# Ending a copy kernel on TensorE in place of SyncE

## The chip, the cores and the metric

The kernel runs on one core of one Trainium2 chip. The metric is the device time of one execution in microseconds (us). The core has five engines that run programs of their own and meet only at semaphores: PE (TensorE), DVE (VectorE), ACT (ScalarE), POOL (GpSimd) and SP (SyncE). Copies are issued by an engine and carried out by 16 DMA engines.

## What is computed

The reference keeps the tokens whose position lies under a capacity and sets the others to zero:

```python
batch, seq, hidden, capacity = 16, 1024, 512, 256
x = np.random.randn(batch, seq, hidden).astype(np.float32)
token_positions = np.random.randint(0, capacity, (batch, seq)).astype(np.int32)

mask = token_positions < capacity
out = (x * mask[..., np.newaxis]).astype(np.float32)
```

`x` and the output have 16 x 1024 x 512 float32 values, 33.55 MB each. The positions of these inputs are all under the capacity, so no token is dropped and the output equals `x`.

## The kernel before

The 16,384 rows of 512 values are spread over 128 partitions of 128 rows each. The kernel copies all of `x` to the output at once, within HBM, and looks meanwhile whether any token has to be dropped.

*The copies (lines 72 to 94).* Eight DMAs of 4 MB each go from `x` to the output, issued in turn by SP and ACT, four by each; ACT first issues the load of the positions into `tp`. All eight count on one semaphore, `s_copy`, by 16 each, so it stands at 128 when all have landed. These issues are moved by hand to the head of the program, ahead of the start-up barriers.

*The check (lines 97 to 127).* DVE computes `keep`, one number of 1 or 0 for each token, from the two 32-bit halves of each position (`ge`, `lt`, `low`, `keep`), and sums it to `kept`. PE adds the 128 partial sums by one matmul with `ones` into `total`, and DVE turns that into `drop_i`: 1 if any token is dropped. The matmul is the only thing that PE does.

*The branch (lines 130 to 161).* SP, ACT and DVE load `drop_i` into a register and branch. If a token is dropped, they load, multiply and store everything again. With these inputs the branch is not taken.

*The end (lines 165 to 175).* [...] ACT and DVE add 1 to `s_done`; SP waits for 2 and adds 1; POOL waits for 3 and clears all of the kernel's semaphores other than `s_copy`. SP at last waits until `s_copy` has 128 and subtracts 128, in one instruction, which the profile books on line 175. No engine but SP waits for the copies on the path that is taken here; the other engines have ended their programs by then. There is no scheduler: the order on each engine is the order in which the code is written.

Of the kernel before, what the change touches and what calls it, by code (L numbers as in the profile page):

```python
# [1 line left out]

# [4 lines left out]


@with_exitstack
def kernel(  # L10
    ctx: ExitStack,
    tc: tile.TileContext,
    x: bass.AP,
    token_positions: bass.AP,
    capacity: bass.AP,
    out: bass.AP,
):
    nc = tc.nc
    P = nc.NUM_PARTITIONS
    fp32 = mybir.dt.float32  # L20
    i32 = mybir.dt.int32
    Alu = mybir.AluOpType

    x_f = x.flatten_outer_dims()
    out_f = out.flatten_outer_dims()
    N, D = x_f.shape
    n_per_p = N // P
    cap = float(int(capacity))
    x_r = x_f.rearrange("(p n) d -> p n d", p=P)
    out_r = out_f.rearrange("(p n) d -> p n d", p=P)  # L30
    tp_i32 = token_positions.rearrange("b s -> (b s)").bitcast(i32)

    sp = nc.sync
    act = nc.scalar
    ve = nc.vector
    pe = nc.tensor
    gp = nc.gpsimd


    tc.close()  # L40
    tc.compile()  # L41

    def sbuf(name, shape, dtype):
        return ctx.enter_context(nc.sbuf_tensor(name, shape, dtype)).ap()

    tp = sbuf("tp", [P, 2 * n_per_p], i32)
    ge = sbuf("ge", [P, n_per_p], fp32)
    lt = sbuf("lt", [P, n_per_p], fp32)
    low = sbuf("low", [P, n_per_p], fp32)
    keep = sbuf("keep", [P, n_per_p], fp32)  # L50
    kept = sbuf("kept", [P, 1], fp32)
    ones = sbuf("ones", [P, 1], fp32)
    drop_i = sbuf("drop_i", [1, 1], i32)
    total = ctx.enter_context(nc.psum_tensor("total", [1, 1], fp32)).ap()
    F = 16
    NBUF = 2
    n_fix = n_per_p // F
    xts = [sbuf(f"xt{b}", [P, F, D], fp32) for b in range(NBUF)]

    s_copy = nc.alloc_semaphore("s_copy")  # L60
    s_tp = nc.alloc_semaphore("s_tp")
    s_ve = nc.alloc_semaphore("s_ve")
    s_pe = nc.alloc_semaphore("s_pe")
    s_ld = [nc.alloc_semaphore(f"s_ld{b}") for b in range(NBUF)]
    s_mul = nc.alloc_semaphore("s_mul")
    s_st = [nc.alloc_semaphore(f"s_st{b}") for b in range(NBUF)]
    s_done = nc.alloc_semaphore("s_done")

    n_copy = 0
    early = []  # L70

    load_tp = act.dma_start(out=tp, in_=tp_i32.rearrange("(p w) -> p w", p=P))
    early.append(load_tp.then_inc(s_tp, 16).ins)

    C = 16
    for k in range(n_per_p // C):
        ins = (sp, act)[k % 2].dma_start(
            out=out_r[:, k * C : (k + 1) * C, :], in_=x_r[:, k * C : (k + 1) * C, :]  # L80
        ).then_inc(s_copy, 16)
        early.append(ins.ins)
        n_copy += 1


    home = nc.cur_bb.bb
    first_bb = nc.cur_f.blocks[0]
    first_sp = next(
        k for k, i in enumerate(first_bb.instructions) if i.engine == mybir.EngineType.SP
    )  # L90
    names = [i.name for i in early]
    home.instructions = [i for i in home.instructions if i.name not in names]
    first_bb.instructions = (
        first_bb.instructions[:first_sp] + early + first_bb.instructions[first_sp:]
    )

    lo = tp[:, 0 : 2 * n_per_p : 2]
    hi = tp[:, 1 : 2 * n_per_p : 2]


    ve.memset(ones, 1.0).then_inc(s_ve, 1)  # L101
    ve.wait_ge(s_tp, 16)
    ve.tensor_scalar(  # L103
        out=ge, in0=lo, scalar1=0.0, scalar2=None, op0=Alu.is_ge
    ).then_inc(s_ve, 1)
    ve.wait_ge(s_ve, 2)
    ve.scalar_tensor_tensor(  # L107
        out=lt, in0=lo, scalar=cap, in1=ge, op0=Alu.is_lt, op1=Alu.mult
    ).then_inc(s_ve, 1)
    ve.wait_ge(s_ve, 3)  # L110
    ve.scalar_tensor_tensor(  # L111
        out=low, in0=hi, scalar=0.0, in1=lt, op0=Alu.is_equal, op1=Alu.mult
    ).then_inc(s_ve, 1)
    ve.wait_ge(s_ve, 4)
    ve.scalar_tensor_tensor(  # L115
        out=keep, in0=hi, scalar=0.0, in1=low, op0=Alu.is_lt, op1=Alu.add
    ).then_inc(s_ve, 1)
    ve.wait_ge(s_ve, 5)
    ve.tensor_reduce(  # L119
        out=kept, in_=keep, axis=mybir.AxisListType.X, op=Alu.add  # L120
    ).then_inc(s_ve, 1)
    pe.wait_ge(s_ve, 6)
    pe.matmul(out=total, lhsT=ones, rhs=kept, start=True, stop=True).then_inc(s_pe, 1)  # L123
    ve.wait_ge(s_pe, 1)
    ve.tensor_scalar(  # L125
        out=drop_i, in0=total, scalar1=float(N) - 0.5, scalar2=None, op0=Alu.is_lt
    ).then_inc(s_ve, 1)


    for e in (sp, act, ve):  # L130
        e.wait_ge(s_ve, 7)
    ET = mybir.EngineType
    drop = nc.values_load(
        drop_i[0:1, 0:1],
        engines=[ET.SP, ET.Activation, ET.DVE],
        min_val=0,
        max_val=1,
        skip_runtime_bounds_check_because="a comparison gives 0 or 1",
    )
    with nc.If(drop):  # L140
        for u in range(n_fix):
            b = u % NBUF
            if u >= NBUF:
                sp.wait_ge(s_st[b], 16 * (u // NBUF))
            sp.dma_start(out=xts[b], in_=x_r[:, u * F : (u + 1) * F, :]).then_inc(s_ld[b], 16)
            ve.wait_ge(s_ld[b], 16 * (u // NBUF + 1))
            for j in range(F):
                c = u * F + j
                ve.tensor_scalar(
                    out=xts[b][:, j, :],  # L150
                    in0=xts[b][:, j, :],
                    scalar1=keep[:, c : c + 1],
                    scalar2=None,
                    op0=Alu.mult,
                ).then_inc(s_mul, 1)
            if u == 0:
                act.wait_ge(s_copy, 16 * n_copy)
            act.wait_ge(s_mul, (u + 1) * F)
            act.dma_start(out=out_r[:, u * F : (u + 1) * F, :], in_=xts[b]).then_inc(s_st[b], 16)
        for b in range(NBUF):  # L160
            act.wait_ge(s_st[b], 16 * (n_fix // NBUF))

    for e in (act, ve):
        e.sem_inc(s_done, 1)
    sp.wait_ge(s_done, 2)
    sp.sem_inc(s_done, 1)
    own = [s_tp, s_ve, s_pe, *s_ld, s_mul, *s_st, s_done]
    ids = sorted(s.num for s in own)  # L170
    assert ids == list(range(ids[0], ids[-1] + 1))
    gp.wait_ge(s_done, 3)
    gp.sem_clear(range(ids[0], ids[-1] + 1))
    sp.wait_ge(s_copy, 16 * n_copy)
    sp.sem_inc(s_copy, -16 * n_copy)


# [1 line left out]
_INS = ['x', 'token_positions', 'capacity']  # L179
_OUTS = [((16, 1024, 512), 'float32')]  # L180

_NUMBERS = {'capacity': 256}


# [26 lines left out]
```

## Time and profile before

| what | value |
|---|---|
| median of 4 runs | 105.85 us (105.61 to 106.36) |
| profiled execution | 105.69 us |
| its span, first to last instruction of the program | 104.4 us |
| busy: PE, DVE, POOL | 0.2, 1.5 and 0.2 us |
| moved in HBM | 33.69 MB read, 33.55 MB written |
| mean granted TensorE clock | 1.000 |

The page counts only computing instructions as busy; issues of DMAs, branches and semaphore instructions are not in its table of groups, but stand in the views by line under names such as SPq or PEldq (the queue of an engine's sequencer; PEldq is PE's). Times inside the profile count from the first instruction of the program. What an engine does ahead of its program and behind it has no rows there; the trace keeps the updates of every semaphore, those too that fall outside the span.

### The profile page before, as it was taken

Reading aid. Unit: us, or ns where it says so; the run is one execution under the profiler, and the core shown is the slowest. Engines: PE = TensorE matmul, PEld = TensorE weight load, DVE = VectorE, ACT = ScalarE, POOL = GpSimd, SP = SyncE. Lnnn points to the kernel's source line nnn. Section 1 sums busy time; section 2 is a strip of 40 time slices with the busy share of each in tenths; the row PEclk is TensorE's granted clock in tenths of the full one; section 3 lists DMA queues with packets and bytes.
Section 4 is the critical chain, followed back from the end, with each engine's and each line's share of the span. In section 5 each row is a group of like instructions: output and inputs, shape, how many; then the busy total and the mean of one; then the engine's idle time right before and its main releaser. Section 6 shows DMA issues by size and latency. Waiting matters only on the chain. (4 is left out here: it accounts for less than half of the span.)

```text
span 104.4 us, 70 instructions
## 1 busy us (share of the span) xinstructions
PE 0.2 (0%) x2; PEld 0.1 (0%) x2; DVE 1.5 (1%) x7; POOL 0.2 (0%) x4
## 2 busy tenths in 40 slices
PE   0000000000000000000000000000000000000000
PEld 0000000000000000000000000000000000000000
DVE  0230000000000000000000000000000000000000
POOL 0000000000000000000000000000000000000000
DMA  7997989979989899889799698997998998998974
GB/s 251 402 352 264 364 279 352 377 239 389 314 289 402 276 327 402 289 314 377 264 364 402 214 389 264 339 377 251 377 339 276 389 339 264 402 301 301 402 251 151
DMA packets 1297, 33.69 MB, mean 323 GB/s; under 512 B 144, under 2 KB 272, under 8 KB 272
## 3 DMA queue, kind: packets, MB, share of 16 engines
q10 hardware_dynamic: 720, 16.91, 49.7%
q1 hardware_dynamic: 576, 16.78, 48.2%
q14 instruction: 1, 0.01, 0.0%
HBM read 33.69 MB, written 33.55 MB: 644 GB/s over the span
## 5 line engine op out<-in xcount | busy, mean ns | idle before, releaser
L115 DVE SCALAR_TENSOR_TENSOR keep<-tp,low 128x128 f32<-128x128 int32 x1 | 0.3, 293 | 0.0
L107 DVE SCALAR_TENSOR_TENSOR lt<-tp,ge 128x128 f32<-128x128 int32 x1 | 0.3, 291 | 0.0
L111 DVE SCALAR_TENSOR_TENSOR low<-tp,lt 128x128 f32<-128x128 int32 x1 | 0.3, 291 | 0.0
L119 DVE TENSOR_REDUCE kept<-keep 128x1 f32<-128x128 f32 x1 | 0.3, 286 | 0.0
L103 DVE TENSOR_SCALAR ge<-tp 128x128 f32<-128x128 int32 x1 | 0.2, 227 | 0.0
L123 PE MATMUL total<-kept,ones 128*1 128x1 f32 x2 | 0.2, 164 | 6.1 <-DVE kept L119 6.1
L125 DVE TENSOR_SCALAR drop_i<-total 1x1 int32<-1x1 f32 x1 | 0.1, 147 | 0.3 <-PE total L123 0.3
L101 DVE MEMSET ones<- 128x1 f32 x1 | 0.1, 59 | 4.5 <-PEq L41 4.5
L192 POOL MEMSET const-bfloat16-1.0<- 128x1 bf16 x1 | 0.1, 103 | 0.0
L192 POOL MEMSET const-uint8-127<- 128x1 uint8 x1 | 0.1, 102 | 0.0
L192 POOL MEMSET const-float32-1.0<- 128x1 f32 x1 | 0.1, 100 | 0.0
L192 POOL MEMSET const-float32-0.0<- 128x1 f32 x1 | 0.1, 99 | 0.2 <-issue 0.2
L123 PEld LDWEIGHTS total<-kept,ones 128*1 128x1 f32 x2 | 0.1, 80 | 6.1 <-DVE kept L119 6.1
## 6 DMA issues: line engine op xcount, KB each, us to landing
out_dram<-in_x_dram SPq DMA_DIRECT2D x4, 4096.0 KB, 62.2
out_dram<-in_x_dram ACTq DMA_DIRECT2D x4, 4096.0 KB, 67.7
tp<-in_token_positions_dram ACTq DMA_DIRECT2D x1, 128.0 KB, 2.3
```

The source lines that it names most:

```text
L101: ve.memset(ones, 1.0).then_inc(s_ve, 1)
L103: ve.tensor_scalar(out=ge, in0=lo, scalar1=0.0, scalar2=None, op0=Alu.is_ge).then_inc(s_ve, 1)
L107: ve.scalar_tensor_tensor(out=lt, in0=lo, scalar=cap, in1=ge, op0=Alu.is_lt, op1=Alu.mult).then_inc(s_ve, 1)
L111: ve.scalar_tensor_tensor(out=low, in0=hi, scalar=0.0, in1=lt, op0=Alu.is_equal, op1=Alu.mult).then_inc(s_ve, 1)
L115: ve.scalar_tensor_tensor(out=keep, in0=hi, scalar=0.0, in1=low, op0=Alu.is_lt, op1=Alu.add).then_inc(s_ve, 1)
L119: ve.tensor_reduce(out=kept, in_=keep, axis=mybir.AxisListType.X, op=Alu.add).then_inc(s_ve, 1)
L123: pe.matmul(out=total, lhsT=ones, rhs=kept, start=True, stop=True).then_inc(s_pe, 1)
L125: ve.tensor_scalar(out=drop_i, in0=total, scalar1=float(N) - 0.5, scalar2=None, op0=Alu.is_lt).then_inc(s_ve, 1)
L192: nc = _bacc.Bacc("TRN2", target_bir_lowering=False, num_devices=1)
```

## The change

The last part of the program is moved from SP to PE. SP now adds 1 to `s_done` like ACT and DVE. PE waits for 3 and adds 1, POOL waits for 4 in place of 3, and PE in place of SP waits until `s_copy` has 128 and subtracts 128.

```diff
-    for e in (act, ve):
+    for e in (sp, act, ve):
         e.sem_inc(s_done, 1)
-    sp.wait_ge(s_done, 2)
-    sp.sem_inc(s_done, 1)
+    pe.wait_ge(s_done, 3)
+    pe.sem_inc(s_done, 1)
     own = [s_tp, s_ve, s_pe, *s_ld, s_mul, *s_st, s_done]
     ids = sorted(s.num for s in own)
     assert ids == list(range(ids[0], ids[-1] + 1))
-    gp.wait_ge(s_done, 3)
+    gp.wait_ge(s_done, 4)
     gp.sem_clear(range(ids[0], ids[-1] + 1))
-    sp.wait_ge(s_copy, 16 * n_copy)
-    sp.sem_inc(s_copy, -16 * n_copy)
+    pe.wait_ge(s_copy, 16 * n_copy)
+    pe.sem_inc(s_copy, -16 * n_copy)
```

## The prediction

> **What bounds the kernel now.** I read the page first, then the DMA view, the stretches at the end, SP's own waits, and the views of the lines that hold semaphore instructions. The page and the DMA view:
>
> ```profile
> span 104.4 us, 70 instructions
> ...
> DMA  7997989979989899889799698997998998998974
> ...
> q10 hardware_dynamic: 720, 16.91, 49.7%
> q1 hardware_dynamic: 576, 16.78, 48.2%
> ...
> HBM read 33.69 MB, written 33.55 MB: 644 GB/s over the span
> ```
>
> The two queues that carry the eight copies take 49.7% and 48.2%, 97.9% together, of what 16 DMA engines have in the span. No compute engine comes to 2%. The kernel is a copy from HBM to HBM, and everything else hides behind it. The page's chain of waits stops at 6.5 us, where the vector work ends, because it follows compute instructions; what ends the program stands in SP's own waits:
>
> ```profile
> SPq L175 <- SPq L175: 96.6, 1, 96.6
> ...
> SPq L168 <- SPq L168: 0.7, 1, 0.7
> ```
>
> For 96.6 us SP stands in its last instruction, the wait for the copies (the profile's L175, lines 174 and 175 in one instruction). The lines that issue and end the program, by line:
>
> ```profile
> DMA to landing us min/median/max: 24.8/65.0/101.9
> ...
> L175 SPq EVENT_SEMAPHORE  x1: 17/17/17, 104.3 to 104.3; - x1
> ...
> L173 POOLq EVENT_SEMAPHORE_RANGE_CLEAR  x1: 92/92/92, 7.7 to 7.7; - x1
> ```
>
> The slowest copy lands 101.9 us after its issue at 2.5 us, so near 104.3; SP wakes and its 17 ns instruction is the last of the span. POOL had cleared the other semaphores at 7.7 us. So the change can touch only two things: the few nanoseconds between the last landing and the end of the program, and what follows the program. The profiled execution is told as 105.69 us with a span of 104.35 (104.4 on the page), so 1.34 us lie outside the span, and they are not idle. The trace's record of semaphore updates goes on behind L175. In us from the span's start: a semaphore that the kernel doesn't own, number 2, is updated at 104.484, 104.527, 104.565, 104.600 and 104.647; then the other semaphores are cleared one by one, up to 105.220; then number 2 is updated nine more times, from 105.444 to 105.800. It was also updated at 6.477, 7.342, 8.364 and 8.408, and nine times ahead of the span, from -0.379 to -0.009.
>
> I read this as a barrier that passes through the five engines in a fixed order and back: five arrivals and four returns, nine updates. The order can be read from who could have arrived. At 6.477 only PE had finished its program (matmul ended at 6.303). At 7.342 ACT had (7.198). At 8.364 and 8.408 DVE (7.678) and POOL (7.838) had. SP, ending at 104.352, is the fifth. So PE is first in the row, ACT second, SP last, the turning point.
>
> **The change part by part.** The built program of after has on PE two more instructions behind its matmul (wait for s_done and increment; wait for s_copy and subtract 128) and on SP one plain increment in their place. Nothing else moves: the copies, their issue from SP and ACT and all compute are in the same order on their engines.
>
> *The hand-shake at 7 us.* SP, ACT and DVE now all increment; PE waits for three and increments to four; POOL waits for four. PE has nothing queued behind that but the wait for the copies. POOL's clear comes some 0.05 us later, PE's slower instruction. The cover is the copy, from 7.8 to 104.3 us, 96 us. I cost this at nothing; uncovered it would be those 0.05 us. SP's end comes earlier, about 7.7 us; it had no DMA left to issue.
>
> *Wake after the last landing.* SP's L175 started 16 ns after the last update of s_copy (104.319 to 104.335). PE wakes more slowly: in the three barriers at the start PE started 28 to 29 ns after the releasing update, SP 17. +12 ns.
>
> *The instruction itself.* From the view of line 41:
>
> ```profile
> L41 SPq EVENT_SEMAPHORE  x2: 17/17/17, 4.1 to 4.4; - x2
> ...
> L41 PEldq EVENT_SEMAPHORE  x2: 51/51/51, 4.1 to 4.4; - x2
> ```
>
> 51 ns on PE against 17 on SP: +34 ns. [...]
>
> *From the program's end to the first barrier update.* SP took 132 ns (104.352 to 104.484). PE took 174 ns from the end of its matmul (6.303 to 6.477), ACT 144 (7.198 to 7.342). PE behind a semaphore instruction, at the end of a long wait, isn't shown. Nearest row: PE's own 174, less about 10 because the matmul's end is modelled; +35 ns. Bounds: below, an exit like SP's, 0; above, POOL's, which ended at 7.838 and was not through the row before 8.364, 526 ns, so +394 ns. A gain is excluded here: no engine left in under 132 ns.
>
> *The barrier itself.* In before only SP was missing, the last of the row, and five updates took 163 ns (104.484 to 104.647). With PE missing nobody passes until PE has come: the second, third and fourth arrivals wait parked, and all nine updates run after it. The row for that is the same semaphore's full rounds: 370 ns ahead of the span (-0.379 to -0.009) and 356 ns behind the clears (105.444 to 105.800). So +193 to +207 ns; I take +200. [...]
>
> *Behind the barrier.* The last update of it releases PE in both kernels (first in, last out). PE's clears are the slowest block: semaphores 7 to 53 fall from 104.873 to 105.220, while those from 207 on are through by 104.685. So the clears start from PE's release as before, and the 1.15 us from there to 105.800 stay as they are.
>
> The sum: 12 + 34 + 35 + 200 = 281 ns, +0.28 us, from +0.24 (exit and round at their low ends) to +0.65 (both high). On the profiled execution, 105.69 becomes 105.97. That execution lies 0.16 below the median of the four runs, so for a median I add to 105.85: **106.13**. That is +0.27%, inside the 0.5% (0.53 us) that a measurement of this kernel can tell from no change, since its four runs alone spread from 105.61 to 106.36.
>
> **The rivals.**
>
> *PE is slow to leave (slower).* One mechanism at one place: the step from PE's last instruction to its barrier arrival. For it: POOL's step was 526 ns, the profile shows nothing of what an engine does there, and PE was never seen doing it at the end of a 96 us wait. Against it: PE itself was through in 174 ns, and SP left in 132 after just such a wait. At POOL's price the sum is +0.65: 106.50. It decides from an exit of about 0.42 us, where 0.246 of the other terms and 0.28 of extra exit make 0.53.
>
> *The tail isn't in the time.* If what is told as the time ended with the span plus a constant, only wake and instruction count: +0.05, 105.90. For it: the records behind the program sum to 1.45 us (104.352 to 105.800), the time outside the span is 1.34, so the two don't match exactly. Against it: nothing else in the trace could fill 1.34 us.
>
> *The copies run differently.* With SP through its program early and PE parked instead, the copies might end earlier or later. Nothing in the profile speaks for it: all eight are issued by 3.1 us, the stretch from 5 to 95 us has DMA shares of 1.00 and 0.99, and no engine takes part. The runs' own spread prices it: the fastest lies 0.24 below the median and the slowest 0.51 above; with the new tail that gives 105.9 to 106.6, and to be faster by over 0.5% the copies would have to shorten by 0.81 us.
>
> ```profile
> 5.00:50.00 45.00, 0.19 (x2) 0.09 (x2) 1.10 (x5) 0.00 (x0) 1.00 1.00 328
> 50.00:95.00 45.00, 0.00 (x0) 0.00 (x0) 0.00 (x0) 0.00 (x0) 1.00 0.99 326
> ...
> 103.00:104.00 1.00, 0.00 (x0) 0.00 (x0) 0.00 (x0) 0.00 (x0) 1.00 0.01 0
> ```
>
> (columns: stretch, us, busy time of PE, its weight loads, DVE and POOL, granted clock, DMA share, GB/s.) The last row also shows why no engine's speed can help: data has stopped by 103, and the last completions come up to 104.32 on their own.
>
> That the change doesn't do what it says is ruled out by the built program, where PE's last instruction is the wait for 128.
>
> **How the numbers follow.** Forecast (+0.28): 0.55, of which the scatter of a median over few runs, some 0.2 us, puts 0.08 beyond +0.53. Slow exit: 0.25, of which 0.19 beyond. Tail not counted: 0.10, nearly all within 0.5%. Copies changed: 0.10, half faster, the rest mostly slower. Together slower 0.31, within 0.5% 0.63, faster 0.06. The range runs from 105.75, the tail-not-counted case less most of that scatter, to 106.60, the slow exit with a little of it.
>
> **What would show it.** In the changed kernel's profile: the wait of 96 us under PE and none of that length under SP; PE's last instruction of 51 ns; a span longer by about 0.05 us if the copies take the same. In the semaphore updates: number 2 silent from the start of the program to about 104.56, then nine updates in 0.36 us instead of five in 0.16, and the clears behind them unchanged in length. An update of number 2 before PE ends would refute the order I read; a gap over 0.42 us ahead of the first would make the slow exit right; a time outside the span still at 1.34 us would mean that the tail isn't counted.

## The result, and the profile after

The changed kernel took 106.19 us (median of 52 runs, 105.70 to 106.83), the kernel before in the same comparison 105.87 (78 runs, 105.44 to 106.71). The ratio is 1.003, with a 95% interval of 1.0019 to 1.0041: 0.32 us slower, 0.20 to 0.43 by the interval. The forecast was 106.13, +0.28.

The profiled execution of after took 105.79 us with a span of 104.12 (104.1 on the page). Its page:

```profile
span 104.1 us, 71 instructions
...
q10 hardware_dynamic: 720, 16.91, 49.7%
q1 hardware_dynamic: 576, 16.78, 48.5%
...
HBM read 33.69 MB, written 33.55 MB: 646 GB/s over the span
```

The copies are the bound as before: the two queues that carry them take 98.2% of what 16 DMA engines have in the span. In this execution they ended earlier, so the span is shorter by 0.23 us, and the execution is longer all the same. The views by line show where the end now stands:

```profile
DMA to landing us min/median/max: 24.9/65.3/101.6
...
L166 SPq EVENT_SEMAPHORE  x1: 17/17/17, 7.2 to 7.2; - x1
...
L168 PEldq EVENT_SEMAPHORE  x1: 51/51/51, 7.7 to 7.7; - x1
...
L175 PEldq EVENT_SEMAPHORE  x1: 51/51/51, 104.1 to 104.1; - x1
```

SP's last instruction is now its increment at 7.2 us, PE's takes 51 ns and ends the span. SP's own waits have lost the 96.6 us on L175; the view of waits lists none for PE in their place, since it books a waiting semaphore instruction for SP alone. All of SP's waits in after:

```profile
SPq L133 <- DVE drop_i L125: 2.1, 1, 2.1
SPq L192 <- PEq L192: 0.5, 1, 0.5
SPq L41 <- PEq L41: 0.5, 2, 0.3
```

What the views can't show is behind the span, in the trace's record of semaphore updates. Semaphore 2, us from the start of the span, with everything from the program's first instruction on:

```
before   6.477  7.342  8.364  8.408
         104.484 104.527 104.565 104.600 104.647
         105.444 105.478 105.516 105.560 105.583 105.681 105.720 105.754 105.800
after    104.403 104.437 104.475 104.519 104.543 104.641 104.679 104.714 104.760
         105.546 105.580 105.619 105.662 105.685 105.784 105.822 105.856 105.903
```

Four early updates and five late ones have become nine late ones. The way from the last landing to the last update can be cut into five pieces, for every kernel of this study alike. All but the times of the runs are from one profiled execution each, in ns:

| kernel | wake | last instruction | leaving | updates behind the end | their time | rest | sum |
|---|---|---|---|---|---|---|---|
| before (SP ends) | 16 | 17 | 132 | 5 | 163 | 1153 | 1481 |
| after (PE ends) | 29 | 51 | 279 | 9 | 357 | 1143 | 1859 |
| e_act (ACT ends) | 21 | 17 | 145 | 8 | 323 | 1153 | 1659 |
| e_dve (DVE ends) | 27 | 21 | 183 | 6 | 241 | 1151 | 1623 |
| e_pool (POOL ends) | 25 | 17 | 561 | 7 | 285 | 1152 | 2040 |
| e_shake (SP ends) | 16 | 17 | 132 | 5 | 163 | 1146 | 1474 |

Wake is from the last landing of a copy to the start of the waiting instruction; leaving is from the program's end to the next update of semaphore 2; rest is the clears and the second barrier. After less before is 1859 - 1481 = 378 ns, inside the measured 0.20 to 0.43 us.

Part of this can be seen in more than the profiled executions, since many runs have their span on record, to 0.1 us. Time less span was 1.28 to 1.38 us in 52 runs of before and 1.62 to 1.72 us in 54 of after, with means of 1.33 and 1.66. The table has for the same stretch, the last three pieces together, 1448 and 1779 ns: 0.33 us more in both ways.

### The profile page after: what moved, and what is told of

It reads as the page before. It is cut to its first block, busy times and chain, and to the rows that moved or that the text cites. A ratio compares the mean times of both kernels' runs of the same rounds, so it can differ in the third digit from the quotient of the medians.

```text
span 104.1 us, 71 instructions
## 1 busy us (share of the span) xinstructions
PE 0.2 (0%) x2; PEld 0.1 (0%) x2; DVE 1.5 (1%) x7; POOL 0.2 (0%) x4
```

## The experiments

Theory: when the program has ended, the engines pass a barrier in a fixed row, PE, ACT, POOL or DVE, SP, and back. An engine that is through early stands parked in its place; what follows the engine that is late, the leaving of that engine and all later places of the row, is paid. Rivals: it costs that SP isn't last, whichever engine takes its place; the long wait makes PE slow; what follows the span isn't in the time.

**Other engines at the end: e_act, e_dve, e_pool.** The same move, to another engine:

```diff
-    for e in (act, ve):
+    for e in (sp, ve):
         e.sem_inc(s_done, 1)
-    sp.wait_ge(s_done, 2)
-    sp.sem_inc(s_done, 1)
+    act.wait_ge(s_done, 2)
+    act.sem_inc(s_done, 1)
...
-    sp.wait_ge(s_copy, 16 * n_copy)
-    sp.sem_inc(s_copy, -16 * n_copy)
+    act.wait_ge(s_copy, 16 * n_copy)
+    act.sem_inc(s_copy, -16 * n_copy)
```

In e_dve it is `ve` (the first loop over `sp, act`). In e_pool `sp`, `act` and `ve` increment, and `gp` waits for 3, clears, and then waits for the copies.

> ACT waits for the copies and ends the program. Barrier order (ACT second in the row): the nine updates of semaphore 2 split into one early, by PE, and eight behind ACT's end; ACT wakes and runs like SP (17 ns), leaves in about 0.14 us, and the eight updates take 0.32 us (the 0.357 of the round in after, less its first step of 0.034). From last landing to last update about 1.65 us, against 1.48 in before and 1.86 in after: a time about 0.17 us over before. The rival, that any engine but SP in last place costs alike: nine updates behind the end, or at least the same +0.32 us as in after.

> DVE waits for the copies and ends the program. Barrier order (DVE third or fourth in the row): two or three updates early, seven or six behind DVE's end, which take 0.24 to 0.29 us; DVE's instruction is 21 ns and its wake 27; its leaving isn't known, 0.13 to 0.28 us. From last landing to last update 1.57 to 1.76 us: +0.1 to +0.25 us over before. The rival, that any engine but SP costs alike: +0.32 us.

> POOL waits for the copies and ends the program, behind its clear of the other semaphores. Barrier order (POOL third or fourth): two or three updates early, seven or six behind POOL's end, 0.24 to 0.29 us. POOL's leaving is the open price: about 0.15 us behind a plain semaphore instruction gives +0.1 us over before, the up to 0.53 us that it took behind the clear in before gives +0.5. The rival, that any engine but SP costs alike: +0.32 us.

Measured: e_act 105.92 us against 105.69 of before, ratio 1.0029 (1.0010 to 1.0049); e_dve 105.73, ratio 1.0020 (0.9997 to 1.0043); e_pool 106.16, ratio 1.0062 (1.0036 to 1.0087). (These ratios and intervals come from all the runs; they are not the quotients of the medians beside them.) By the table's sums they should be 0.178, 0.142 and 0.559 us over before, ratios of 1.0017, 1.0013 and 1.0053, each inside its interval. The times of e_act and e_dve can't be told from one another, nor from +0.32 us; the counts in their traces can. Semaphore 2 from the program's start to the end of the first barrier, us, with a bar where the program ended (104.183, 104.766 and 103.927):

```
e_act    6.505 | 104.328 104.366 104.410 104.434 104.531 104.570 104.604 104.651
e_dve    6.644 7.508 8.511 | 104.949 104.972 105.070 105.109 105.143 105.190
e_pool   6.477 7.342 | 104.488 104.532 104.555 104.654 104.692 104.726 104.773
```

Eight late updates with ACT, seven with POOL and six with DVE settle the order: PE, ACT, POOL, DVE, SP. The rival that any engine but SP costs alike expected nine, or +0.32 us each, and falls: time less span, in all the runs, is on average 0.19, 0.13 and 0.57 us over before (by the table 0.173, 0.127 and 0.550), where after has 0.33. POOL's price is its leaving, 561 ns behind a plain semaphore instruction of the usual length, so the clear ahead of it in before wasn't the reason for its slow step. The last instruction in e_pool, and in e_dve, by line:

```profile
L173 POOLq EVENT_SEMAPHORE  x1: 17/17/17, 103.9 to 103.9; - x1
```

```profile
L175 DVEq EVENT_SEMAPHORE  x1: 21/21/21, 104.7 to 104.7; - x1
```

**PE and SP both late: e_both.** On top of the kernel before, PE waits for the copies and SP for PE:

```diff
+    pe.wait_ge(s_copy, 16 * n_copy)
+    pe.sem_inc(s_copy, 16)
-    sp.wait_ge(s_copy, 16 * n_copy)
-    sp.sem_inc(s_copy, -16 * n_copy)
+    sp.wait_ge(s_copy, 16 * n_copy + 16)
+    sp.sem_inc(s_copy, -16 * n_copy - 16)
```

> PE waits for the copies and adds 16 to s_copy; SP waits for that and subtracts all, so SP has the last instruction and PE ends late too. Barrier order: PE is first in the row, so nobody passes before PE has left; SP is through (17 + 17 + 132 ns behind PE's update) before PE's own first barrier update (0.28 us behind its instruction). Nine updates behind the end, and a time like that of after, +0.3 to +0.4 us over before. The rival, that it costs because SP isn't last: a time like before plus the extra hand-over, +0.1 us at most, and five updates behind SP's end.

Measured: 106.05 us against 105.69, ratio 1.0051 (1.0034 to 1.0068). The two last instructions, by line:

```profile
L175 PEldq EVENT_SEMAPHORE  x1: 51/51/51, 104.2 to 104.2; - x1
...
L177 SPq EVENT_SEMAPHORE  x1: 17/17/17, 104.3 to 104.3; - x1
```

SP ends the program, at 104.273, and yet nine updates follow, the first at 104.506: that is 279 ns behind PE's instruction, as in after. From the last landing to the last update it is 1860 ns, after's 1859. So the price hangs on PE being late, not on SP being absent.

**Half of the change: e_shake.** PE does the hand-shake as in after; SP waits for the copies as in before:

```diff
-    for e in (act, ve):
+    for e in (sp, act, ve):
         e.sem_inc(s_done, 1)
-    sp.wait_ge(s_done, 2)
-    sp.sem_inc(s_done, 1)
+    pe.wait_ge(s_done, 3)
+    pe.sem_inc(s_done, 1)
...
-    gp.wait_ge(s_done, 3)
+    gp.wait_ge(s_done, 4)
```

> Half of the change: PE does the hand-shake at 7.7 us (one semaphore instruction as its last), SP waits for the copies and ends the program. In time: 0, like before, since 96 us cover the hand-shake; the rival that PE in the hand-shake or SP's place in it costs expects a part of the +0.32 us. The open point is why PE took 279 ns to leave in after: if leaving behind a semaphore instruction is that dear on PE, the first barrier update comes 0.28 us behind PE's instruction near 7.7 us, here too; if the 96 us wait made it dear, it comes after 0.17 us, as behind the matmul in before.

Measured: 105.58 us against 105.75, ratio 0.9985 (0.9966 to 1.0005), no difference. The sum of its pieces is 1474 ns against 1481. So the second half of the change, the wait for the copies, carries all of the cost. PE's last instruction here:

```profile
L168 PEldq EVENT_SEMAPHORE  x1: 51/51/51, 7.7 to 7.7; - x1
```

It ends at 7.764, and the first update of semaphore 2 follows at 8.042: 278 ns, after a wait of 1.4 us at most. The long wait is not what makes PE slow to leave. ACT had ended its program at 7.190, but its update, which came at 7.342 in before, follows PE's by 34 ns at 8.076: nobody passed before PE.

**A matmul ahead of leaving: e_pe_mm.** As after, with one more line at the end, a repeated matmul whose result nobody uses:

```diff
+    pe.matmul(out=total, lhsT=ones, rhs=kept, start=True, stop=True)
```

> As the changed kernel, but PE does its matmul once more behind the wait for the copies (one more matmul than the reference needs, its result unused). If part of PE's leaving runs while the matmul is still in the array, leaving takes 0.17 us from the matmul's end as in before, and the matmul (two passes, about 0.19 us) costs clearly less than its own time: nothing to +0.1 us over after. If the long wait made leaving dear, it takes about 0.28 us from the matmul's end, and the time is 0.2 us over after.

Measured: 106.01 us against 105.75 of before, ratio 1.0036 (1.0013 to 1.0060). The added matmul, by line:

```profile
L176 PEld LDWEIGHTS total<-kept,ones x2: 79/80/81, 104.2 to 104.2; 128*1 128x1 f32 x2
L176 PE MATMUL total<-kept,ones x2: 163/164/164, 104.2 to 104.2; 128*1 128x1 f32 x2
```

From PE's semaphore instruction (end 104.168) to the end of the matmul (104.414) pass 246 ns, and from there only 148 to the first update, where 0.17 us was expected. Together 394, against 279 without the matmul: 246 ns of work cost 115. The sum from landing to last update is 1985, +126 over after, a little over the +0.1 that was expected. So some 130 ns of the way out run beside the matmul. The forecast's price, the 174 ns of before from the end of PE's matmul, left such a part out. What PE does in that time, and whether it belongs to the semaphore instruction or to the leaving, no run shows.

**Ten more semaphore instructions: e_pe_ten and e_sp_ten.** On the engine that ends the program, behind its wait:

```diff
+    for k in range(10):
+        pe.sem_inc(s_copy, 1 if k % 2 == 0 else -1)
```

(`sp` in e_sp_ten, on top of the kernel before.)

> As the changed kernel, with ten more semaphore instructions on PE behind the wait (adding and taking away 1 in turn). At 51 ns each: span and time +0.51 us over after, +0.83 us over before, and leaving 0.28 us as in after. If PE's 51 ns overlap one another, less. [...]

> As the kernel before, with ten more semaphore instructions on SP behind the wait. At 17 ns each: +0.17 us over before, more if an issue gap stands between them; five barrier updates behind the end as in before. If the ten cost as much here as on PE, the 51 ns of PE are not what the instruction costs on the path.

Measured: e_pe_ten 107.95 us against 105.75, ratio 1.0220 (1.0185 to 1.0255), of four runs; e_sp_ten 106.06, ratio 1.0040 (1.0014 to 1.0065). Both expectations missed in time; five updates follow in e_sp_ten, as expected, and nine in e_pe_ten. The ten, on PE and on SP (busy time of one, first and last start in us):

```profile
L177 PEldq EVENT_SEMAPHORE  x10: 51/51/51, 104.6 to 106.0; - x10
```

```profile
L177 SPq EVENT_SEMAPHORE  x10: 17/17/17, 104.4 to 104.9; - x10
```

The busy times are 51 and 17, but the starts are farther apart: on PE 104.644 to 106.001 is nine steps of 151 ns, on SP 104.402 to 104.934 nine steps of 59. So in such a sequence a semaphore instruction costs an engine the instruction and a gap, about 100 ns on PE and 42 on SP, that no view shows. The gap doesn't stand ahead of every instruction: in e_pe_mm PE's weight load starts 26 ns behind the end of its semaphore instruction. And behind the ten, PE leaves in 234 ns, not in the 279 of after that were expected; why is open. SP leaves in 131, as in before. From landing to last update the sums are 3399 and 2075 ns, 1918 and 594 over before. The second, a ratio of 1.0056, lies in its interval; the first, 1.0181, lies just under it. Time less span is 0.31 us over before in the four runs of e_pe_ten (by the same pieces of its trace 0.32), so what is missing lies inside the span; four runs are too few to say whether it is more than the scatter of the copies.

## Why the prediction was right, and where a term was off

- *The hand-shake costs nothing.* Right: e_shake, 0.9985 (0.9966 to 1.0005). SP ended its program at 7.2 us in after, not at about 7.7; nothing hung on it.
- *Wake, +12 ns.* 29 against 16: +13.
- *The instruction, +34 ns.* 51 ns on PE against 17 on SP in every kernel: right as a duration. In succession the difference is larger, as ten start 151 against 59 ns apart (e_pe_ten, e_sp_ten).
- *Leaving, +35 ns, from 0 to +394.* This term of the sum was mis-sized: 279 against 132, +147 ns. The row for it, PE's 174 ns behind a matmul, was the nearest by engine but not by instruction: beside a matmul part of the way out is covered (e_pe_mm, 148 ns left), behind a semaphore instruction it was 278 ns (e_shake). The 10 ns taken off for the modelled end has no row behind it, and 174 - 10 - 132 is 32, not 35. The upper bound, POOL's step, was not PE's case.
- *The barrier, +193 to +207 ns.* 357 against 163: +194. The order that was read from the early updates held, and e_act, e_dve and e_pool add the places of POOL and DVE in it. The steps in after are 34, 38, 44, 24, 98, 38, 35 and 46 ns. The first four, 140 ns, are the extra ones; and the step back from SP takes 98 where all have just come through, but 43 in before, where DVE's update was 96 us old: 55 more.
- *Behind the barrier, 0.* 1143 against 1153: -10; with SP at the end it was 1153 in one execution and 1146 in another (e_shake). The last of the semaphores from 207 on falls at 104.687 in before, not by 104.685; nothing changes by it.
- *The sum.* +0.281 was forecast; the pieces give +0.378 and the runs +0.32 (0.20 to 0.43). The result stays within 0.5%, as the likeliest case had it. That 106.13 came within 0.06 us of 106.19 is partly luck: the leaving was short by 0.11 us, and the medians differ by 0.06 less than the pieces, which the scatter of the copies covers. The time outside the span shows the shortfall: +0.33, where the forecast's leaving and barrier make 0.235.

Of the rivals: *slow to leave* had the right step but not its price, 0.28 us where it needed 0.42 to decide. *The tail isn't in the time* is refuted: in all ten profiled executions the last update of semaphore 2, counted from the span's start, lies 0.10 to 0.12 us above the time told for that execution (before 105.80 and 105.69, after 105.90 and 105.79, e_pe_ten 107.82 and 107.72), though the span differs between them by up to 2.1 us and the time outside it by 0.56. Outside the span are 1.67 us in after, not 1.34. *The copies run differently* found nothing for it: in ten profiled executions their last landing lies between 103.89 and 104.72 us, with no order by kernel. The runs bound it: 54 spans of after have a mean of 104.55 us; the 78 times of before have one of 105.90, which less 1.33 makes a span of 104.57. Less wake and last instruction, 0.08 and 0.03, the copies ended 0.07 us earlier in after, give or take 0.10 (95%). That is an estimate, as the spans of these 78 runs are not on record; a shift of a tenth of a microsecond could still hide in it.

No version here beats the kernel before. SP is the last in the barrier's row (five updates behind its end, against six to nine), leaves soonest (132 ns against 145 to 561) and has, with ACT and POOL, the shortest instruction (17 ns against 21 on DVE and 51 on PE), so of the five engines it was the cheapest to be late.

## What to carry to other kernels

In this program the engine that finishes last paid for its own way out and for every place behind it in the barrier that follows the program, so the last wait belongs on the engine that is last in that row and quick to leave; here that is SP, and the choice among the five is worth up to 0.56 us by the profiled executions (e_pool). Semaphore updates behind the span show this in one profile, where the times of runs need dozens. A row used as a price should match the instruction as well as the engine: PE's way out was 174 ns behind a matmul in before and 279 behind a semaphore instruction in after; e_pe_mm showed some 130 ns of it running beside the matmul.

## What the runs showed of the hardware that was not expected

Ten semaphore instructions in succession start 151 ns apart on PE, of which 51 are shown as busy (e_pe_ten), and 59 apart on SP, of which 17 are shown (e_sp_ten); a weight load on PE started 77 ns behind the start of one (e_pe_mm). From the end of the semaphore instruction that waits for the copies to the first update of the barrier, POOL took 561 ns (e_pool), PE 279 (after), DVE 183 (e_dve), ACT 145 (e_act) and SP 132 (before); behind ten more such instructions PE took 234 (e_pe_ten), and behind a matmul 174 (before) and 148 (e_pe_mm).
